# Token-major products written into the recurrence's steps, and Ln with Exp on ScalarE for the powers of three norms

## The chip, the cores and the metric

The kernel runs on one core of a Trainium2 chip, on one sequence of 512 tokens with 1024 features, in float32. The metric is the device time of one execution in microseconds (us); lower is better. A core's engines have queues of their own and each works through its queue in order: PE (TensorE, matrix products; PEld is its loading of weights), DVE (VectorE), ACT (ScalarE), POOL (GpSimd) and SP, which here only starts DMAs. An engine waits for another by semaphores.

## What is computed

Two networks run one after the other, each of two layers. The change concerns the second one, whose layer has a hybrid mixer: sliding-window attention, a gated linear recurrence (`hgrn2`) and a gated delta rule, fed by one projection, and their outputs joined by another. Cut to the norms that the change touches:

```python
def rmsnorm_2(x, gain):          # x / sqrt(mean(x*x) + eps), times (a gain)
def l2norm(x):                   # x / sqrt(sum(x*x) + eps)

def hybrid_mixer(h, ...):
    aq, ak, av, bq, bf, bv, bg, cqkv, cg, cb, ca = jnp.split(h @ w_in, split_at, axis=-1)
    ...                                          # attention on aq, ak, av
    o_b = hgrn2_chunked(bq, log_f, bv)
    out_b = rmsnorm_2(o_b, hgrn_norm) * jax.nn.silu(bg)
    cq, ck, cv = ...                             # silu of a causal convolution of cqkv
    cq = l2norm(cq) * (C_DK ** -0.5)
    ck = l2norm(ck)
    o_c = gated_delta_chunked(cq, ck, cv, beta, g)
    out_c = rmsnorm_2(o_c, gdn_norm) * jax.nn.silu(cg)
    return jnp.concatenate([out_a, out_b, out_c], axis=-1) @ w_out
```

Every one of these norms needs a power -1/2 of a few columns: 128 tokens by 4, 8 or 32 values.

## The kernel before

All activations of a layer stay in the core's memory. Weights stream in by DMA, 128 rows of a matrix at a time (`wraw`). Every large product is made of three products of reduced-precision parts, so that it comes near float32: ACT casts the weights to a high part `whi` (L381), DVE subtracts it to get the low part `wlo` (L382), and PE adds up high times high (L406), low times high (L407) and high times low (L408) in one accumulator. Feature-major products (features on partitions, `lin_f`) do this for one output tile of 128 features with 24 matmuls of 512 columns; the token-major ones (tokens on partitions, `lin_t`, lines L475 to L477) do it with the activations as the moving side. A scheduler sets the order on each engine: it takes operations in the order in which they are written, as a priority, but lets later ones go ahead where its model of the time says that an earlier one would wait. The program that comes out is fixed; the queues don't reorder it.

One hybrid layer is written out by `second_mixer` (L1707 to L1771). It makes four feature-major tiles, then starts the recurrence (`hgrn`, a generator whose steps the caller asks for) between the 512-column token-major products of `win2_t0`; runs the steps to their end; makes the 392-column products of `win2_t1` (their results leave by `evt1`, L1741); makes the five tiles of queries and keys for the attention (each is evicted as `u` at L1721, squared at L663, and the square summed by eight two-column products at L1724); makes six tiles for the delta rule, with a causal convolution and a tanh (L832 to L844); and then weaves the delta rule (`gdn`) with the attention (`swa`). The output projection, `w_out`, follows; its first input tiles are ready early, and its products fill PE beside the delta rule's last blocks.

Three norms take their power on POOL:

- The recurrence's output norm: `hgrn` calls `head_rstd` (L1019) for each of two pairs of heads. ACT copies the result out of PSUM (`ho`, L1332) and squares it (`hsq`, L1024), DVE sums and scales it (`hms`, L1026, L1030), POOL raises 8 columns to -1/2 (`pw`, L669), and DVE multiplies (L1334, L1335).
- The norms of the delta rule's queries and keys: PE sums squares with two-column products (L1379), DVE adds the epsilon (`gms`, L1381), POOL raises three groups of columns (`grn`, L1384); ACT spreads them over 64 columns each (`sp`, L682), PE transposes the spread (L676), and DVE multiplies the two key tiles with it (L1390). The queries' part goes into `grq` (L1394).
- The delta rule's output norm, once for each of four blocks of 128 tokens: `hsq` on ACT, `hms` on DVE (L1026 to L1030, with `grq` squared into it), the power of 4 columns on POOL (L669), two products on DVE (L1033, L1567), and two transposes on PE (L1569) that put the block into the tiles from which the output projection's last inputs are cast (`hi`, L399).

Of the kernel before, what the change touches and what calls it, by code (L numbers as in the profile page):

```python
# [12 lines left out]
AF = mybir.ActivationFunctionType  # L13
ALU = mybir.AluOpType
# [3 lines left out]
P = 128  # L18
SEQ = 512
NB = SEQ // P  # L20
# [229 lines left out]
class Net:  # L250
# [415 lines left out]
    def pow_half(self, x, n):  # L666
# [2 lines left out]
        self.nc.gpsimd.tensor_tensor(r, x, self.nhalf[:, 0:n], op=ALU.pow)  # L669
        return r  # L670

    def spread(self, cols):

        ps = self.ps()
        for b in range(NB):
            self.nc.tensor.transpose(ps[:, b * P:(b + 1) * P], cols(b), self.ident)  # L676
        return ps
# [338 lines left out]

        last.append(lambda: finish(*late.pop(0), "mm"))

    def head_rstd(self, x, shape, pre=None):  # L1019

        V = self.nc.vector
        a, b = shape
        sq = self.t((P, a, b, 64), name="hsq")
        self.nc.scalar.activation(out=sq, in_=x, func=AF.Square)  # L1024
        ms = self.small((P, a, b), f"hms{a}{b}", 2)
        V.tensor_reduce(ms, sq, axis=AX.X, op=ALU.add)  # L1026
        if pre is not None:
            V.tensor_tensor(ms, ms, pre, op=ALU.mult)
            V.tensor_tensor(ms, ms, pre, op=ALU.mult)
        V.tensor_scalar(ms, ms, 1.0 / 64, EPS, op0=ALU.mult, op1=ALU.add)  # L1030
        r = self.pow_half(ms.rearrange("p a b -> p (a b)"), a * b).rearrange("p (a b) -> p a b", a=a)
        if pre is not None:
            V.tensor_tensor(r, r, pre, op=ALU.mult)  # L1033
        return r
# [175 lines left out]
    def hgrn(self, q, z, v, bg, l, last):  # L1210
        nc, V, G = self.nc, self.nc.vector, self.nc.gpsimd
# [38 lines left out]
        def pair(i):  # L1250
# [79 lines left out]
                        nc.tensor.matmul(o, w, x, start=n == 0, stop=n == len(terms) - 1)  # L1330
            hs = self.t((P, NB, 2, 64), name="ho")
            nc.scalar.copy(hs, ps.rearrange("p (a b c) -> p b a c", a=2, b=NB))  # L1332
            r = self.head_rstd(hs, (NB, 2))
            V.tensor_tensor(hs, hs, bg[:, :, i * P:(i + 1) * P].rearrange("p a (b c) -> p a b c", b=2), op=ALU.mult)  # L1334
            V.tensor_tensor(hs, hs, r.unsqueeze(3).to_broadcast([P, NB, 2, 64]), op=ALU.mult)  # L1335
            done[i] = hs
# [9 lines left out]
    def gdn(self, x, cg, ba, l, out):  # L1346
        nc, V, G = self.nc, self.nc.vector, self.nc.gpsimd
# [20 lines left out]
        f = lambda y: y.rearrange("p a b -> p (a b)")  # L1368
# [10 lines left out]
                T.matmul(st[:, 8 * b + 2 * i:8 * b + 2 * i + 2], sq[:, b * P:(b + 1) * P], self.bd64[:, 0:65:64], start=True, stop=True)  # L1379
        rs_ = self.small((P, 32), "gms", 2)  # L1380
        V.tensor_scalar(rs_, st[:, 0:32], EPS, None, op0=ALU.add)  # L1381
        rs3, rn = rs_.rearrange("p (a b) -> p a b", a=NB), self.small((P, NB, 8), "grn", 2)
        def power(c):
            G.tensor_tensor(rn[:, :, c], rs3[:, :, c], self.nhalf[:, 0:32].rearrange("p (a b) -> p a b", a=NB)[:, :, c], op=ALU.pow)  # L1384

        power(slice(4, 6))
        power(slice(6, 8))
        for i in range(2, 4):
            ps = early.spread2(rn[:, :, 2 * i:2 * i + 2])
            V.tensor_tensor(x[i], x[i], ps, op=ALU.mult)  # L1390
            yield
        power(slice(0, 4))
        rq = self.small((P, NB, 4), "grq", 2)
        V.tensor_scalar(rq, rn[:, :, 0:4], 0.125, None, op0=ALU.mult)  # L1394
        q, k, vf = x[0:2], x[2:4], x[4:6]
# [147 lines left out]
        for b in range(NB):  # L1543
            s = slice(b * P, (b + 1) * P)
            un, hs = self.t((P, 4, 64), name="gvn", tag="x"), self.t((P, 1, 4, 64), name="go", tag="x")
            po = self.ps("mx")
            o3 = lambda y: y.rearrange("p (a b) -> p a b", a=4)
            if b == 0:
                V.tensor_copy(un, uw[b][:, :, 0:64])
            else:  # L1550
                for i in range(2):
                    T.matmul(po[:, i * P:(i + 1) * P], wt[i][:, s], sbd[b][:, i, :], start=True, stop=True)
                    T.matmul(po[:, 256 + i * P:256 + (i + 1) * P], q[i][:, s], sbd[b][:, i, :], start=True, stop=True)
                V.tensor_tensor(un, uw[b][:, :, 0:64], o3(po[:, 0:256]), op=ALU.subtract)
            p2 = self.ps("mx")
            for h in range(4):
                T.matmul(p2[:, h * 64:(h + 1) * 64], QT[b][:, h, :], un[:, h, :], start=True, stop=True)
            if b == 0:
                V.tensor_copy(hs[:, 0], o3(p2[:, 0:256]))
            else:  # L1560
                t = self.t((P, 4, 64), name="got", tag="x")
                V.tensor_tensor(t, o3(po[:, 256:512]), eg[:, b, :].unsqueeze(2).to_broadcast([P, 4, 64]), op=ALU.mult)
                V.tensor_tensor(hs[:, 0], t, o3(p2[:, 0:256]), op=ALU.add)
            r = self.head_rstd(hs, (1, 4), rq[:, b:b + 1, :])
            h3 = hs[:, 0]
            V.tensor_tensor(h3, h3, o3(cg[:, b, :]), op=ALU.mult)
            V.tensor_tensor(h3, h3, r.rearrange("p a b -> p (a b)").unsqueeze(2).to_broadcast([P, 4, 64]), op=ALU.mult)  # L1567
            for i in range(2):
                T.transpose(yt[i][:, s], h3[:, 2 * i:2 * i + 2, :].rearrange("p a b -> p (a b)"), self.ident)  # L1569
            yield  # L1570
# [136 lines left out]
    def second_mixer(self, x, l):  # L1707
# [47 lines left out]
        for n, _ in enumerate(self.lin_t_steps(self.d["win2_t0"][l], x, 512, evt0)):  # L1755
            if n + 1 in (7, 8):
                next(gh)
        for n, _ in enumerate(gh):
            if n == 2:
                gains(bg, "hgrn_norm")  # L1760
        self.lin_t(self.d["win2_t1"][l], x, 392, evt1)
        gains(cg, "gdn_norm")
        self.lin_f(w[10:15], x, lambda o, ps: ev(o + 10, ps))
        ga = self.using("l", "mx").swa([keep[o] for o in range(10, 14)], keep[14], keep["st"], av, l, self.tab2, y_a)
# [71 lines left out]
def drain(gen):  # L1836
    for _ in gen:
        pass
# [25 lines left out]
```

## Time and profile before

| | |
|---|---|
| time, median of 3 runs | 3589.97 us (3586.79 to 3591.79) |
| profiled execution, its own time | 3586.55 us |
| its span, first to last instruction | 3584.7 us |
| busy: PE, DVE, ACT, POOL | 97%, 55%, 38%, 4% of the span |
| mean granted TensorE clock | 0.992 of full speed |

The span is the recorded stretch of the profiled execution; its time is a little longer by what lies around it. Busy time is an average over stages with different limits, so the views by stretch (windows) and by instruction (timeline) say more than the shares. In the timeline a row may hold several like instructions (x8), and a bracket tells how long the engine had been idle before and what ended that.

### The profile page before, as it was taken

The page shows a single profiled execution, that of the slowest core. Times are in us where ns is not written, and L with a number is a line of the kernel's source. Part 1 is how long each engine was busy: PE and PEld are TensorE (multiplying, and loading weights), DVE is VectorE, ACT ScalarE, POOL GpSimd, SP SyncE. Part 2 cuts the span into 40 slices and gives each one's busy share as a digit, 9 for nine tenths or more (in the row PEclk, how much of TensorE's full clock was granted, in tenths as well). Part 3 has the DMA queues.
Part 4 walks back from the last instruction along what each step waited for, and adds up shares of the span by engine and source line. Part 5 has one row for each costly group of instructions (what it writes and reads, how often), then busy time and mean ns, then how long its engine had stood idle before and what let it go on. Part 6 is the DMA issues. An engine that isn't in the chain of part 4 may idle for free.

```text
span 3584.7 us, 44503 instructions
## 1 busy us (share of the span) xinstructions
PE 3484.3 (97%) x17694; PEld 2901.8 (81%) x17694; DVE 1989.1 (55%) x3074; ACT 1364.5 (38%) x2231; POOL 140.5 (4%) x130
## 2 busy tenths in 40 slices
PE   9999999999999999999999998899999989999999
PEld 7888777888888888777888887788888877888887
DVE  6555665554665555674556577756333475654333
ACT  4223454323333223463223364354222453543221
POOL 0000000000000000000000003100000021000000
PEclk9999999999999999999999999899999999999999
DMA  5444212444334443202444321102333222022332
GB/s 167 141 135 129 84 32 68 142 145 128 127 100 142 146 138 100 91 15 95 146 148 137 94 77 54 62 7 75 108 98 101 78 71 68 1 71 90 100 99 83
DMA packets 114272, 349.06 MB, mean 97 GB/s; under 512 B 11536, under 2 KB 27920, under 8 KB 114064
## 3 DMA queue, kind: packets, MB, share of 16 engines
q1 hardware_dynamic: 114064, 346.21, 30.8%
q8 instruction: 140, 2.29, 0.3%
q14 instruction: 68, 0.56, 0.0%
HBM read 339.87 MB, written 2.10 MB: 95 GB/s over the span
## 4 chain that ended last, share of the span: by engine, by line
PE 87%; DVE 6%; issue 3%; ACT 2%; POOL 1%; DMA 1%; SPq 0%; POOLq 0%; DVEq 0%; ACTq 0%
PE mm L406 24%; PE mm L408 24%; PE mm L407 24%; PE mm L1481 1%; PE mm L1476 1%; PE mm L476 1%; PE mm L477 1%; PE mm L475 1%; PE mx L968 1%; DVE hacc L1279 1%; DVE wlo L382 1%; PE mm L809 1%; PE mx L948 1%; ACT sc L1138 1%; PE mx L1121 1%
## 5 line engine op out<-in xcount | busy, mean ns | idle before, releaser
L381 ACT CAST whi<-wraw 128x1024 fp32r<-128x1024 f32 (+3 forms) x540 | 553.4, 1029 | 1553.6 <-PE mm L407 1271.7
L406 PE MATMUL mm<-xh,whi 128*128 128x512 f32 (+1 forms) x2784 | 1053.3, 380 | 9.7 <-ACT whi L381 6.4
L407 PE MATMUL mm<-xl,whi 128*128 128x512 f32 (+1 forms) x2784 | 1055.8, 380 | 1.6 <-DVE xl L588 1.4
L408 PE MATMUL mm<-xh,wlo 128*128 128x512 f32 (+1 forms) x2784 | 1055.8, 380 | 0.3 <-DVE wlo L382 0.3
L382 DVE TENSOR_TENSOR wlo<-wraw,whi 128x1024 fp32r<-128x1024 f32 (+3 forms) x540 | 643.7, 1194 | 274.9 <-ACT whi L381 234.3
L406 PEld LDWEIGHTS mm<-xh,whi 128*128 128x128 f32 x2784 | 522.4, 189 | 107.8 <-ACT whi L381 6.4
L407 PEld LDWEIGHTS mm<-xl,whi 128*128 128x128 f32 x2784 | 524.9, 189 | 100.3 <-DVE xl L588 2.5
L408 PEld LDWEIGHTS mm<-xh,wlo 128*128 128x128 f32 x2784 | 524.8, 189 | 100.4 <-DVE wlo L382 3.1
L408 PE MATMUL mm<-hi,wlo 128*128 128x512 f32 (+1 forms) x1390 | 532.2, 383 | 2.1 <-DVE wlo L382 2.1
L406 PE MATMUL mm<-hi,whi 128*128 128x512 f32 (+1 forms) x1390 | 532.5, 384 | 0.2
L407 PE MATMUL mm<-lo,whi 128*128 128x512 f32 (+1 forms) x1390 | 531.8, 383 | 0.0
L408 PEld LDWEIGHTS mm<-hi,wlo 128*128 128x128 f32 x1390 | 261.3, 188 | 54.2 <-DVE wlo L382 4.2
L406 PEld LDWEIGHTS mm<-hi,whi 128*128 128x128 f32 x1390 | 261.1, 188 | 51.4 <-ACT hi L399 1.1
L407 PEld LDWEIGHTS mm<-lo,whi 128*128 128x128 f32 x1390 | 261.3, 188 | 50.3
L658 DVE SCALAR_TENSOR_TENSOR h<-mm,h 128x512 f32<-128x512 f32 x112 | 77.2, 691 | 224.2 <-PE mm L408 224.1
L1589 DVE SCALAR_TENSOR_TENSOR ada<-wraw,cond,ada 128x1024 f32<-128x1024 f32 x84 | 107.9, 1284 | 95.6 <-DMA wraw<-in_ada_w_dram 95.2
L637 DVE TENSOR_TENSOR gl<-mm,rstd 128x512 f32<-128x512 f32 x88 | 60.7, 690 | 155.1 <-PE mm L408 155.1
L636 DVE TENSOR_TENSOR silu<-mm,rstd 128x512 f32<-128x512 f32 x88 | 60.7, 689 | 145.2 <-PE mm L408 145.2
L658 DVE SCALAR_TENSOR_TENSOR h<-mm,mod,h 128x512 f32<-128x512 f32 (+1 forms) x70 | 48.9, 704 | 148.7 <-PE mm L408 148.7
L399 ACT CAST hi<-gl 128x512 fp32r<-128x512 f32 x132 | 82.2, 623 | 100.6 <-DVE gl L639 99.9
L633 DVE TENSOR_TENSOR gl<-silu,mm 128x512 f32<-128x512 f32 x44 | 30.2, 687 | 135.8 <-PE mm L408 135.8
L400 DVE TENSOR_TENSOR lo<-gl,hi 128x512 fp32r<-128x512 f32 x132 | 90.5, 686 | 15.4 <-ACT hi L399 15.4
(493 smaller groups left out, 3606.2 us busy)
## 6 DMA issues: line engine op xcount, KB each, us to landing
wraw<-in_ffn_gate_dram SPq DMA_DIRECT2D x130, 512.0 KB, 3.5
wraw<-in_ffn_up_dram SPq DMA_DIRECT2D x130, 512.0 KB, 4.0
wraw<-in_ada_w_dram SPq DMA_DIRECT2D x96, 512.0 KB, 3.7
wraw<-in_ffn_down_dram SPq DMA_DIRECT2D x96, 448.0 KB, 3.3
wraw<-in_win_f_dram SPq DMA_DIRECT2D x50, 512.0 KB, 3.5
wraw<-in_ffn_down_dram SPq DMA_DIRECT2D x48, 512.0 KB, 3.5
wraw<-in_w_out_dram SPq DMA_DIRECT2D x32, 512.0 KB, 3.5
wraw<-in_win_t_dram SPq DMA_DIRECT2D x16, 512.0 KB, 3.5
```

The costliest lines, as they stand in the source:

```text
L381: self.nc.scalar.copy(hi[:, s], raw)
L382: self.nc.vector.tensor_tensor(lo[:, s], raw, hi[:, s].bitcast(F32), op=ALU.subtract)
L399: self.nc.scalar.copy(hi, src)
L400: self.nc.vector.tensor_tensor(lo, src, hi.bitcast(F32), op=ALU.subtract)
L406: T.matmul(ps, whi, xhi, start=first, stop=False)
L407: T.matmul(ps, whi, xlo, start=False, stop=False)
L408: T.matmul(ps, wlo, xhi, start=False, stop=last)
L475: T.matmul(ps, xh[:, bs], w[0][:, s], start=k == 0, stop=False)
L636: nc.vector.tensor_tensor(sg, gate_ps, rb, op=ALU.mult)
L637: nc.vector.tensor_tensor(gg, up_ps, rb, op=ALU.mult)
L658: self.nc.vector.scalar_tensor_tensor(h, ps[:, c], scale, h, op0=ALU.mult, op1=ALU.add)
L1589: V.scalar_tensor_tensor(acc, raw, cond[:, k:k + 1], acc, op0=ALU.mult, op1=ALU.add)
```

## The change

It does two things.

First, the generator of the 392-column products (`t1`) is asked for a step after every second step of the recurrence, and what is left of it is run afterwards. Before, all of it stood behind the recurrence.

Second, a new helper, `exp_half`, computes the power as exp(-ln(x)/2) with two ACT instructions, Ln and Exp with a scale of -0.5. It takes the place of POOL's pow in the three norms above. At the start of the delta rule all 32 columns go through one pair, where POOL had three instructions. `pow_half` stays where other norms use it. ACT's functions come in tables, and the built program has an `ACT_TABLE_LOAD` wherever the next function isn't in the table that is loaded: 29 of them before, 53 after.

```diff
--- before.py
+++ after.py
@@ -667,6 +667,12 @@
 
         r = self.small((P, n), f"pw{n}", 2)
         self.nc.gpsimd.tensor_tensor(r, x, self.nhalf[:, 0:n], op=ALU.pow)
+        return r
+
+    def exp_half(self, x, r):
+
+        self.nc.scalar.activation(out=r, in_=x, func=AF.Ln)
+        self.nc.scalar.activation(out=r, in_=r, func=AF.Exp, scale=-0.5)
         return r
 
     def spread(self, cols):
@@ -1016,7 +1022,7 @@
 
         last.append(lambda: finish(*late.pop(0), "mm"))
 
-    def head_rstd(self, x, shape, pre=None):
+    def head_rstd(self, x, shape, pre=None, power=None):
 
         V = self.nc.vector
         a, b = shape
@@ -1028,7 +1034,10 @@
             V.tensor_tensor(ms, ms, pre, op=ALU.mult)
             V.tensor_tensor(ms, ms, pre, op=ALU.mult)
         V.tensor_scalar(ms, ms, 1.0 / 64, EPS, op0=ALU.mult, op1=ALU.add)
-        r = self.pow_half(ms.rearrange("p a b -> p (a b)"), a * b).rearrange("p (a b) -> p a b", a=a)
+        if power:
+            r = power(ms, self.small((P, a, b), f"hrs{a}{b}", 2))
+        else:
+            r = self.pow_half(ms.rearrange("p a b -> p (a b)"), a * b).rearrange("p (a b) -> p a b", a=a)
         if pre is not None:
             V.tensor_tensor(r, r, pre, op=ALU.mult)
         return r
@@ -1330,7 +1339,7 @@
                         nc.tensor.matmul(o, w, x, start=n == 0, stop=n == len(terms) - 1)
             hs = self.t((P, NB, 2, 64), name="ho")
             nc.scalar.copy(hs, ps.rearrange("p (a b c) -> p b a c", a=2, b=NB))
-            r = self.head_rstd(hs, (NB, 2))
+            r = self.head_rstd(hs, (NB, 2), power=self.exp_half)
             V.tensor_tensor(hs, hs, bg[:, :, i * P:(i + 1) * P].rearrange("p a (b c) -> p a b c", b=2), op=ALU.mult)
             V.tensor_tensor(hs, hs, r.unsqueeze(3).to_broadcast([P, NB, 2, 64]), op=ALU.mult)
             done[i] = hs
@@ -1379,17 +1388,11 @@
                 T.matmul(st[:, 8 * b + 2 * i:8 * b + 2 * i + 2], sq[:, b * P:(b + 1) * P], self.bd64[:, 0:65:64], start=True, stop=True)
         rs_ = self.small((P, 32), "gms", 2)
         V.tensor_scalar(rs_, st[:, 0:32], EPS, None, op0=ALU.add)
-        rs3, rn = rs_.rearrange("p (a b) -> p a b", a=NB), self.small((P, NB, 8), "grn", 2)
-        def power(c):
-            G.tensor_tensor(rn[:, :, c], rs3[:, :, c], self.nhalf[:, 0:32].rearrange("p (a b) -> p a b", a=NB)[:, :, c], op=ALU.pow)
-
-        power(slice(4, 6))
-        power(slice(6, 8))
+        rn = self.exp_half(rs_.rearrange("p (a b) -> p a b", a=NB), self.small((P, NB, 8), "grn", 2))
         for i in range(2, 4):
             ps = early.spread2(rn[:, :, 2 * i:2 * i + 2])
             V.tensor_tensor(x[i], x[i], ps, op=ALU.mult)
             yield
-        power(slice(0, 4))
         rq = self.small((P, NB, 4), "grq", 2)
         V.tensor_scalar(rq, rn[:, :, 0:4], 0.125, None, op0=ALU.mult)
         q, k, vf = x[0:2], x[2:4], x[4:6]
@@ -1561,7 +1564,7 @@
                 t = self.t((P, 4, 64), name="got", tag="x")
                 V.tensor_tensor(t, o3(po[:, 256:512]), eg[:, b, :].unsqueeze(2).to_broadcast([P, 4, 64]), op=ALU.mult)
                 V.tensor_tensor(hs[:, 0], t, o3(p2[:, 0:256]), op=ALU.add)
-            r = self.head_rstd(hs, (1, 4), rq[:, b:b + 1, :])
+            r = self.head_rstd(hs, (1, 4), rq[:, b:b + 1, :], self.exp_half)
             h3 = hs[:, 0]
             V.tensor_tensor(h3, h3, o3(cg[:, b, :]), op=ALU.mult)
             V.tensor_tensor(h3, h3, r.rearrange("p a b -> p (a b)").unsqueeze(2).to_broadcast([P, 4, 64]), op=ALU.mult)
@@ -1755,10 +1758,14 @@
         for n, _ in enumerate(self.lin_t_steps(self.d["win2_t0"][l], x, 512, evt0)):
             if n + 1 in (7, 8):
                 next(gh)
+
+        t1 = self.lin_t_steps(self.d["win2_t1"][l], x, 392, evt1)
         for n, _ in enumerate(gh):
             if n == 2:
                 gains(bg, "hgrn_norm")
-        self.lin_t(self.d["win2_t1"][l], x, 392, evt1)
+            if n % 2:
+                next(t1, None)
+        drain(t1)
         gains(cg, "gdn_norm")
         self.lin_f(w[10:15], x, lambda o, ps: ev(o + 10, ps))
         ga = self.using("l", "mx").swa([keep[o] for o in range(10, 14)], keep[14], keep["st"], av, l, self.tab2, y_a)
```

How the built program's order moves is shown at three places, all in the first hybrid layer; the second has the same. In the rows a name's number tells buffers apart, and line numbers of the changed kernel are 3 to 9 higher.

**ACT, end of the recurrence.** Before: squares of the two head pairs (`ho` to `hsq`), a weight cast, and the eviction and square of the first query tile (`u`, `sq`).

```order
L1024 ACTIVATE hsq_16496<-ho_16494 128x512
L1332 COPY ho_16526<-mx_16505 128x512
L1024 ACTIVATE hsq_16528<-ho_16526 128x512
L381 CAST whi_16935<-wraw_16933 128x1024
L1721 ACTIVATE u_16749<-mm_16724,vecs 128x512
L663 ACTIVATE sq_16751<-mm_16724 128x512
```

After, from the second `ho` on (`hrs` is the power of `hms`):

```order
L1341 COPY ho_16667<-mx_16646 128x512
L674 ACTIVATE hrs_3133_16641<-hms_3132_16638 128x8
L1030 ACTIVATE hsq_16669<-ho_16667 128x512
L675 ACT_TABLE_LOAD
L675 ACTIVATE hrs_3133_16641<-hrs_3133_16641 128x8
L381 CAST whi_16937<-wraw_16935 128x1024
L674 ACT_TABLE_LOAD
L674 ACTIVATE hrs_3138_16674<-hms_3137_16671 128x8
L1724 ACTIVATE u_16751<-mm_16726,vecs 128x512
L675 ACT_TABLE_LOAD
L675 ACTIVATE hrs_3138_16674<-hrs_3138_16674 128x8
L663 ACTIVATE sq_16753<-mm_16726 128x512
```

Four short instructions and three loads have come ahead of `sq`.

**DVE, start of the delta rule.** Before, from the last step of a convolution to `grq`; L1390 are the products with the spread norm:

```order
L1126 TENSOR_REDUCE wm_17265<-sc_17269 128x2
L841 SCALAR_TENSOR_TENSOR cacc_17130<-conv_17128,vecs,cacc_17130 128x511
L1390 TENSOR_TENSOR cout_17053<-cout_17053,mm_17239 128x512
L1390 TENSOR_TENSOR cout_17094<-cout_17094,mm_17259 128x512
L844 SCALAR_TENSOR_TENSOR cout_17135<-cout_17135,cacc_17130 128x512
L837 TENSOR_SCALAR cacc_17171<-conv_17169,vecs 128x512
L1394 TENSOR_SCALAR grq_17273<-grn_17234 128x16
```

After; here the first of these products is L1394, and `sc` are scores of the attention, `geb` and `grq` small factors:

```order
L847 SCALAR_TENSOR_TENSOR cacc_17132<-conv_17130,vecs,cacc_17132 128x511
L1407 TENSOR_TENSOR geb_17286<-gb_17181,geg_17201 128x16
L1133 TENSOR_TENSOR sc_17306<-mx_17303,mats_16876 128x512
L1397 TENSOR_SCALAR grq_17274<-grn_17236 128x16
L1133 TENSOR_TENSOR sc_17327<-mx_17324,mats_16876 128x512
L1135 TENSOR_REDUCE wm_17267<-sc_17306 128x2
L1135 TENSOR_REDUCE wm_17267<-sc_17327 128x2
L850 SCALAR_TENSOR_TENSOR cout_17137<-cout_17137,cacc_17132 128x512
L843 TENSOR_SCALAR cacc_17173<-conv_17171,vecs 128x512
L1133 TENSOR_TENSOR sc_17343<-mx_17340,mats_16876 128x512
L847 SCALAR_TENSOR_TENSOR cacc_17173<-conv_17171,vecs,cacc_17173 128x509
L1394 TENSOR_TENSOR cout_17055<-cout_17055,mm_17241 128x512
```

Ten other operations have moved between the convolution's step and the first product with the norm.

**ACT and PE, tail of the delta rule.** Before, ACT has the squares of the four blocks and then the casts for the output projection:

```order
L1024 ACTIVATE hsq_18413<-go_18404 128x256
L1024 ACTIVATE hsq_18443<-go_18428 128x256
L1024 ACTIVATE hsq_18473<-go_18458 128x256
L1024 ACTIVATE hsq_18503<-go_18488 128x256
L399 CAST hi_18517<-mx_18401 128x512
L399 CAST hi_18521<-mx_18402 128x512
```

After, its first two blocks and the start of the third:

```order
L1030 ACTIVATE hsq_18414<-go_18405 128x256
L674 ACT_TABLE_LOAD
L674 ACTIVATE hrs_3509_18421<-hms_3508_18416 128x4
L675 ACT_TABLE_LOAD
L675 ACTIVATE hrs_3509_18421<-hrs_3509_18421 128x4
L1030 ACTIVATE hsq_18445<-go_18430 128x256
L674 ACT_TABLE_LOAD
L674 ACTIVATE hrs_3517_18452<-hms_3516_18447 128x4
L675 ACT_TABLE_LOAD
L675 ACTIVATE hrs_3517_18452<-hrs_3517_18452 128x4
L1030 ACTIVATE hsq_18476<-go_18461 128x256
```

Each block's square now stands behind the Exp of the block ahead.

PE before, from the transposes of the third block (L1569) over those of the fourth to the projection's next input tile:

```order
L1569 MATMUL mx_18401<-base,go_18458 128x128
L1569 MATMUL mx_18402<-base,go_18458 128x128
L406 MATMUL mm_18550<-hi_17954,whi_18533 128x512
L407 MATMUL mm_18550<-lo_17955,whi_18533 128x512
L408 MATMUL mm_18550<-hi_17954,wlo_18534 128x512
L406 MATMUL mm_18551<-hi_17954,whi_18539 128x512
L407 MATMUL mm_18551<-lo_17955,whi_18539 128x512
L408 MATMUL mm_18551<-hi_17954,wlo_18540 128x512
L406 MATMUL mm_18552<-hi_17954,whi_18545 128x512
L1569 MATMUL mx_18401<-base,go_18488 128x128
L1569 MATMUL mx_18402<-base,go_18488 128x128
L407 MATMUL mm_18552<-lo_17955,whi_18545 128x512
```

PE after, the same (transposes are L1572 here):

```order
L406 MATMUL mm_18557<-hi_17955,whi_18550 128x512
L407 MATMUL mm_18557<-lo_17956,whi_18550 128x512
L1572 MATMUL mx_18402<-base,go_18461 128x128
L1572 MATMUL mx_18403<-base,go_18461 128x128
L408 MATMUL mm_18557<-hi_17955,wlo_18551 128x512
L1572 MATMUL mx_18402<-base,go_18492 128x128
L1572 MATMUL mx_18403<-base,go_18492 128x128
L406 MATMUL mm_18554<-hi_18522,whi_18532 128x512
L406 MATMUL mm_18555<-hi_18522,whi_18538 128x512
```

Of the seven products between the third and the fourth block's transposes, and the two behind, one is left between and none behind; the others, and two from ahead of the third block, stand ahead now. Further up, 13 products stood between the scores of the first block and its transposes, and now 21.

## Rows read from the trace of the kernel before

**Rows 1.** Page, part 1: busy us (share of the span) x instructions.

```profile
PE 3484.3 (97%) x17694; PEld 2901.8 (81%) x17694; DVE 1989.1 (55%) x3074; ACT 1364.5 (38%) x2231; POOL 140.5 (4%) x130
```

**Rows 2.** Windows view: stretch, length; busy PE, PEld, DVE, ACT, POOL; clock, DMA.

```profile
2160.00:2215.00 55.00, 45.19 (x386) 37.03 (x386) 53.35 (x80) 19.92 (x49) 24.28 (x19) 1.00 0.12 39
...
2287.00:2335.00 48.00, 37.82 (x234) 32.71 (x233) 40.00 (x102) 21.73 (x59) 6.54 (x3) 0.79 0.08 26
...
2428.00:2450.00 22.00, 19.70 (x112) 15.52 (x111) 11.40 (x40) 2.75 (x6) 4.03 (x4) 1.00 0.00 1
```

**Rows 3.** Waits of PE, 2160 to 2215: total us, times, longest.

```profile
PE mx L1273 <- DVE hk L1265: 8.0, 12, 2.6
```

**Rows 4.** Timeline of ACT: start, us, engine, line, operation, [idle before <-releaser].

```profile
2216.51 0.22 ACT L852 ACTIVATE gla<-gla 128x16 f32<-128x16 f32 x1
...
2216.74 1.28 ACT L853 ACT_TABLE_LOAD   x1
...
2218.04 0.31 ACT L853 ACTIVATE gla<-gla,one 128x16 f32<-128x16 f32 x1
```

**Rows 5.** Timeline, end of the recurrence, beside the query products.

```profile
2230.71 1.05 ACT L381 CAST whi<-wraw 128x1024 fp32r<-128x1024 f32 x1 [1.32 <-PE mm L407]
...
2231.66 0.68 ACT L1721 ACTIVATE u<-mm,vecs 128x512 f32<-128x512 f32 x1
...
2232.24 0.59 ACT L663 ACTIVATE sq<-mm 128x512 f32<-128x512 f32 x1
...
2232.34 0.39 PE L407 MATMUL mm<-xl,whi 128*128 128x512 f32 x1
...
2232.56 0.39 PE L408 MATMUL mm<-xh,wlo 128*128 128x512 f32 x1
...
2232.89 1.05 PE L1724 MATMUL mx<-base,sq 128*128 128x2 f32 x8
```

**Rows 6.** Timeline, start of the delta rule: power and spread.

```profile
2296.30 6.54 POOL L1384 TENSOR_TENSOR grn<-gms,nhalf 128x8 f32<-128x8 f32 x3 [34.67 <-DVE gms L1381]
...
2298.41 0.62 ACT L682 COPY sp<-grn 128x512 f32<-128x512 f32 x1 [6.29 <-POOL grn L1384]
...
2299.08 1.12 PE L676 MATMUL mm<-base,sp 128*128 128x128 f32 x4 [2.54 <-ACT sp L682]
...
2300.24 0.69 DVE L1390 TENSOR_TENSOR cout<-cout,mm 128x512 f32<-128x512 f32 x1 [2.37 <-PE mm L676]
...
2301.91 0.69 DVE L1390 TENSOR_TENSOR cout<-cout,mm 128x512 f32<-128x512 f32 x1 [0.98 <-PE mm L676]
```

**Rows 7.** Timeline, tail of the delta rule: power, transposes, out-projection.

```profile
2430.49 1.01 POOL L669 TENSOR_TENSOR pw<-hms,nhalf 128x4 f32<-128x4 f32 x1 [9.86 <-DVE hms L1030]
...
2431.54 0.16 DVE L1033 TENSOR_TENSOR pw<-pw,grq 128x4 f32<-128x4 f32 x1 [1.13 <-POOL pw L669]
...
2432.22 0.44 PE L1569 MATMUL mx<-base,go 128*128 128x128 f32 x2 [0.94 <-DVE go L1567]
...
2439.55 0.44 PE L1569 MATMUL mx<-base,go 128*128 128x128 f32 x2
...
2443.12 0.44 PE L1569 MATMUL mx<-base,go 128*128 128x128 f32 x2 [0.15 <-DVE go L1567]
...
2446.30 0.44 PE L1569 MATMUL mx<-base,go 128*128 128x128 f32 x2 [1.11 <-DVE go L1567]
...
2447.30 1.19 PE L406 MATMUL mm<-hi,whi 128*128 128x512 f32 x4
```

**Rows 8.** Timeline of PE (two rows) and windows view (two rows): the clock.

```profile
2162.88 1.16 PE L1273 MATMUL mx<-hq,hk 64*128 64x128 f32 x16 [2.55 <-DVE hk L1265]
...
2287.55 2.82 PE L1379 MATMUL mm<-base,sq 128*128 128x2 f32 x24
...
2291.00:2295.00 4.00, 4.00 (x12) 3.25 (x11) 1.79 (x4) 0.90 (x3) 0.00 (x0) 0.57 0.37 132
...
2298.40:2312.05 13.65, 7.89 (x31) 6.43 (x32) 10.78 (x20) 5.24 (x9) 4.44 (x2) 0.50 0.00 1
```

## The prediction

> **What bounds the kernel now.** I read the page's line of engine shares first. PE is busy 97% of the span [rows 1], so an edit on another engine counts only where PE waits for it, or would. Then the stages of one hybrid layer [rows 2]. In the recurrence (2160 to 2215) PE is busy 45.19 of 55 us and DVE 53.35: DVE is the bound. At the start of the delta rule (2287 to 2335) PE has 37.82 of 48, at its tail (2428 to 2450) 19.70 of 22. Between the first two PE is full. The other hybrid layer shows the same pattern about 737 us later, so every term is worked out for one layer and doubled. The rest of the program, the first network included, is untouched. Last I read, instruction by instruction, the places where a power is taken [rows 5 to 7].
>
> **Interleaving: nothing.** The row to save is PE waiting 8.0 us in 12 pieces on DVE's hk products [rows 3]; 16.0 us in both layers. But the order on PE through the recurrence is the same row for row before and after: the scheduler already puts the 392-column products where a step leaves PE free, and when they are written doesn't alter that. DVE stays full [rows 2]. Cost 0; bounds of 1 us either way, for two small exponentials that change place with one cast.
>
> **The power, in general.** POOL's pow goes (1.01 us for 4 columns, 6.54 for the three at the delta start [rows 6, 7]), and two ScalarE instructions come. A short one takes 0.22 us (0.31 for 16 columns), a table load 1.28 [rows 4]. The built program has a load before the Ln and another before the Exp, in nearly every pair. A load waits for nothing, so the one ahead of Ln runs while ACT waits for the mean square; the one between Ln and Exp can't be hidden, and whatever stands behind in ACT's in-order queue pays for both. A pair therefore costs 0.22 + 1.28 + 0.22 = 1.72 us, plus gaps of 0.02.
>
> The Trainium skill ("ScalarE: Activation LUTs", section "What ACT_TABLE_LOAD costs") puts 1283 ns on a load, which the row shows, and some 1380 ns of drain on top. The row doesn't show that: one instruction ends at 2216.73, the load starts at 2216.74, and the Ln starts 0.02 us after the load's end [rows 4].
>
> **Place A: the recurrence's norm, beside the query products.** Now ACT does the second hsq, idles 1.32 us until a weight buffer is free, casts (2230.71), evicts u (2231.66), squares (2232.24); then PE takes the square into the eight two-column products of L1724 (2232.89) without having waited: its last two matmuls began at 2232.34 and 2232.56, and the next full one could have begun 0.22 to 0.23 later [rows 5]. After, the first Ln stands ahead of the second hsq; load and Exp stand ahead of the cast; load and Ln ahead of u; load and Exp ahead of the square. That is 3 loads of 1.30 with their gaps and 4 short ones of 0.22: 4.78 us ahead of the square, of which the idle 1.32 swallows part: 3.46. PE has one more matmul ahead of L1724 now, 0.23. So PE, which waits for nothing there now, stands still for 3.2 us. DVE's wait for the second power is longer too, but covered by work that is needed a whole product later. Bounds 2.0 (a load less on the path) and 3.5. All that follows on PE up to the delta rule is dense, so nothing gives this back: **+3.2**.
>
> **Place B: start of the delta rule.** After the mean square POOL works 6.54 us from 2296.30; PE waits 2.54 us for the first spread (2299.08), DVE 2.37 and 0.98 for the two products with it [rows 6]. After: Ln at 2296.3, load, Exp done near 2298.1, all 32 columns at once. The q half of the norm comes some 4 us sooner. But the tanh and the copy of a convolution stand ahead of the two spreads on ACT, so the k half comes no sooner (first spread near 2299.1, where it started at 2298.4), and on DVE ten other operations, half of them from behind it, now stand ahead of L1390. DVE's 3.35 us of waiting can be filled with work that it did later, and DVE is what PE waits for in this stage. Bounds: -4 (both idles and a little PE time at half clock saved), +1 (L1390 some 2 us later, and the copies of k behind it). I take the middle of what the two idles could bring: **-2**.
>
> **Place C: tail of the delta rule.** Four blocks follow each other: hsq on ACT, mean on DVE, power, two products on DVE, transposes L1569 on PE. DVE waits 1.13 us for POOL here [rows 7]; the pair takes 1.72 and its handover, 1.85. Also hsq of the next block now stands behind the Exp of this one. I walk the blocks with durations of the rows. Block 0: Ln at 2430.49, where pow began; Exp ends 2432.2; transposes could start at 2432.95. But eight matmuls more stand ahead of them, 1.82 us, begun where PE now idles 0.94: 2433.1 against 2432.22, +0.88. Block 1: everything 0.88 later, plus a pair for a pow, 0.72 and a little: 2441.19 against 2439.55, +1.64. Block 2: its hsq could come at 2439.8 and waits for block 1's Exp until 2440.45, then another pair: 2445.25 against 2443.12, +2.13. Block 3 the same way: 2448.87 against 2446.30, +2.57 [rows 7]. The casts and the products L406 x4 of the out-projection follow as now, 1.00 us later: 2449.87 against 2447.30 [rows 7]. PE has no work to put there: before the last transposes seven matmuls stood between them and the ones before; now one, and none behind. So the end moves by the whole chain: **+2.6**. Bounds 2.0 (three blocks by 0.66) and 3.6 (0.88 and four times 0.7).
>
> **The clock.** After places A and C PE runs dense code, and there the clock matters. TensorE fell from 2.4 to 1.2 GHz after 2.82 us of two-column products at 2287.55 without a gap: mean 0.57 of full speed between 2291 and 2295 [rows 8], that is (1 - 0.57) / 0.5 x 4 = 3.4 us at half. It fell again after the 2.54 us wait at 2296.5, 0.50 for 13.65 us; but it didn't fall after 2.55 us of idling before 2162.88: the recurrence is at 1.00 [rows 2, 6, 8]. At A, PE would idle 3.2 us and then do 1.05 us of two-column products; at C idle 3.2 us, do two transposes, and idle 0.8. Both are longer than any of these stretches, so I expect a fall after each. 3.4 us at half clock costs up to 1.7 us where PE is dense: **+1.5 each**, bounds 0 and 1.7.
>
> **Sum.** A layer: 3.2 + 1.5 - 2 + 2.6 + 1.5 = 6.8; two layers **+13.6 us**. The profiled execution took 3586.55 us, of which 3584.7 are the span; the rest doesn't change. It lies 3.42 us under the median, 3589.97, which I take as the base: 3603.6, rounded to **3603.5 us**. What this kernel's measurement can tell from no change is about 0.2%, 7.2 us.
>
> **Rivals.**
> The clock stays up at A and C. For it: the recurrence idles 2.55 us in one piece without a fall [rows 8]. Against it: A and C are longer, and thin work stands beside the wait. 2 x (3.2 - 2 + 2.6) = +7.6: 3597.6, right at the edge of what can be told.
> Not slower: the delta start pays for the rest. The mechanism is DVE's 3.35 us of waiting for POOL [rows 6]: if all of it is filled, and the stretch at half clock ends sooner with it, B gives 4 a layer; with no clock fall at A and C the sum is 2 x (3.2 - 4 + 2.6) = +3.6: 3593.6, within 0.2%. From 2.2 a layer without falls (5.2 with them) it is no longer slower. Against it: L1390, the step that waited, comes later after the change.
> The interleaving works after all and PE's waits in the recurrence go: 16.0 us less [rows 3] than the forecast, 3587.5, and under 3583 with the better end of B. Against it: PE's order there is unchanged and DVE is full.
> One load serves Ln and Exp. Then the loads of A and C fall away: a pair takes 0.44, less than pow's 1.01 [rows 7], A adds nothing, C gives about 0.6 three times, B 2.5: 2 x (-4.3) = -8.6, 3581. Against it: the built program has a load row for both. The Trainium skill ("ScalarE: Activation LUTs", section "Table sets: the hidden batching unit") says that one set holds both functions and one load does; the order of this program doesn't use that.
> A load empties the engine first, and each of the seven unhidden loads of A and C costs more than 1.28. The gap of 0.02 us around it [rows 4] speaks against it; were a load to cost double, 2 x 7 x 1.28 = +18 more: 3621. With the drain of the page above the sum would be an estimated 19 us more.
>
> **How the numbers follow.** Forecast (a fall at one or both places, B between 0 and -3): 0.59, all slower. Clock stays up: 0.20, half slower, half within 0.2%. Delta start pays: 0.11, within. Interleaving: 0.04, of which 0.03 faster. One load: 0.03, faster. Dearer loads: 0.03, slower. That makes slower 0.72, within 0.22, faster 0.06. Range 3594.5 to 3610: down to where the second and third case lie, up to A and C at their high bounds with full clock costs and 0.5 of gain at B, 2 x (3.5 + 1.7 + 3.6 + 1.7 - 0.5) = 20; it leaves out the last two cases, interleaving and part of the delta start.
>
> **What would show it.** The recurrence (2160 to 2215) with the same PE busy time. At L1724 a PE wait of about 3.2 us for the square on ACT. At the delta start DVE without the two waits for L676, and the stage about 2 us shorter. In the tail L1569's waits grow, with 3 us ahead of the last one. Half-clock windows behind L1724's first group and behind L406 x4. The prediction is wrong if loads are hidden at A, if the scheduler's order gives PE other work than I read, or if the stage from 2287 to 2335 shrinks by more than 4 us.

## The result

The changed kernel takes 3606.99 us (median of 4; 3604.53 to 3610.78), the kernel before 3588.42 in the same comparison: a ratio of 1.0055, 95% interval 1.0042 to 1.0067, so it is slower by 15 to 24 us. The ratio makes 19.7 us; the medians lie 18.6 apart. The profiled execution of the changed kernel took 3604.53 us, its span is 3602.7 us: 18.0 more than before.

The page's engine shares of the changed kernel; PE's busy time has grown by 10 us with as many instructions, POOL has lost 27.5 us and ACT gained 37 [rows 1]:

```profile
PE 3494.7 (97%) x17694; PEld 2911.0 (81%) x17694; DVE 1988.7 (55%) x3074; ACT 1401.2 (39%) x2283; POOL 113.0 (3%) x112
```

**Place A, the recurrence's norm.** The timeline of the changed kernel, ACT from the second `ho` to the square, then PE's group of two-column products that needs it (start, us, engine, line):

```profile
2228.22 0.63 ACT L1030 ACTIVATE hsq<-ho 128x512 f32<-128x512 f32 x1
2228.88 1.28 ACT L675 ACT_TABLE_LOAD   x1
2230.17 0.21 ACT L675 ACTIVATE hrs<-hrs 128x8 f32<-128x8 f32 x1
2230.29 1.04 ACT L381 CAST whi<-wraw 128x1024 fp32r<-128x1024 f32 x1
2231.34 1.28 ACT L674 ACT_TABLE_LOAD   x1
2232.64 0.21 ACT L674 ACTIVATE hrs<-hms 128x8 f32<-128x8 f32 x1
2232.75 0.67 ACT L1724 ACTIVATE u<-mm,vecs 128x512 f32<-128x512 f32 x1
2233.44 1.28 ACT L675 ACT_TABLE_LOAD   x1
2234.73 0.21 ACT L675 ACTIVATE hrs<-hrs 128x8 f32<-128x8 f32 x1
2234.85 0.58 ACT L663 ACTIVATE sq<-mm 128x512 f32<-128x512 f32 x1
...
2235.48 1.86 PE L1727 MATMUL mx<-base,sq 128*128 128x2 f32 x8 [2.84 <-ACT sq L663]
```

The three loads stand where the order had them, and each begins within 0.03 us of the end of the instruction ahead of it. PE waits 2.84 us for the square where it waited for nothing [rows 5]. From the group before to this one it takes 8.07 us, before 4.95.

**Place B, the start of the delta rule.** The timeline there; the first row of DVE is the product with the spread norm, L1390 before [rows 6]:

```profile
2301.47 0.23 ACT L674 ACTIVATE grn<-gms 128x32 f32<-128x32 f32 x1 [2.83 <-DVE gms L1390]
2301.72 1.28 ACT L675 ACT_TABLE_LOAD   x1
...
2303.01 0.23 ACT L675 ACTIVATE grn<-grn 128x32 f32<-128x32 f32 x1
...
2303.92 3.75 PE L1130 MATMUL mx<-kz,u 128*128 128x256 f32 x8 [2.16 <-DVE sc L1133]
...
2304.13 1.14 ACT L688 COPY sp<-grn 128x512 f32<-128x512 f32 x2
...
2307.46 1.91 PE L682 MATMUL mm<-base,sp 128*128 128x128 f32 x8
2308.56 0.69 DVE L1394 TENSOR_TENSOR cout<-cout,mm 128x512 f32<-128x512 f32 x1 [0.68 <-PE mm L682]
```

The power is ready 1.8 us after Ln begins, and DVE's wait for the spread norm has shrunk from 3.35 us to 0.68. But the first product with the norm comes 7.1 us after the power's begin, before 3.9. PE no longer waits for the spread; it waits 2.16 us for DVE's scores now.

**Place C, the tail.** The last block on ACT and DVE, then the four pairs of transposes and the projection's next products [rows 7]:

```profile
2452.09 0.20 ACT L674 ACTIVATE hrs<-hms 128x4 f32<-128x4 f32 x1 [0.22 <-DVE hms L1036]
2452.32 1.28 ACT L675 ACT_TABLE_LOAD   x1
2453.61 0.20 ACT L675 ACTIVATE hrs<-hrs 128x4 f32<-128x4 f32 x1
...
2453.84 0.16 DVE L1042 TENSOR_TENSOR hrs<-hrs,grq 128x4 f32<-128x4 f32 x1 [1.79 <-ACT hrs L675]
...
2439.04 0.41 PE L1572 MATMUL mx<-base,go 128*128 128x128 f32 x2
2447.01 0.44 PE L1572 MATMUL mx<-base,go 128*128 128x128 f32 x2 [0.61 <-DVE go L1570]
2450.98 0.44 PE L1572 MATMUL mx<-base,go 128*128 128x128 f32 x2 [0.54 <-DVE go L1570]
2454.52 0.69 PE L1572 MATMUL mx<-base,go 128*128 128x128 f32 x2 [2.87 <-DVE go L1570]
2455.67 2.07 PE L406 MATMUL mm<-hi,whi 128*128 128x512 f32 x4 [0.46 <-ACT hi L399]
```

DVE waits 1.79 us for the power (1.13 to 1.19 before), and from the first transposes to the last it takes 15.48 us, before 14.08. PE stands still for 2.87 us ahead of the last.

**The clock.** The windows view of the changed kernel, behind A, further behind A, and behind C (the number after the five busy times is the granted clock):

```profile
2234.00:2242.00 8.00, 6.52 (x20) 5.52 (x21) 0.69 (x1) 1.42 (x3) 0.00 (x0) 0.57 0.17 61
2242.00:2246.00 4.00, 4.00 (x23) 3.20 (x22) 1.23 (x1) 2.12 (x3) 0.00 (x0) 1.00 0.09 10
...
2453.50:2461.50 8.00, 6.52 (x19) 4.92 (x20) 1.94 (x5) 1.67 (x5) 0.00 (x0) 0.59 0.00 0
```

At both places TensorE falls to 1.2 GHz: 0.57 over 8 us is (1 - 0.57) / 0.5 x 8 = 6.9 us at half, and 0.59 is 6.6. The product behind A takes 9.19 us from group to group in the first layer, 7.94 in the second, before 6.59 and 6.60: +2.60 and +1.34.

### The profile page after: what moved, and what is told of

The parts are those of the page before. It is cut to its first block, busy times and chain, and to the rows that moved or that the text cites. A ratio compares the mean times of both kernels' runs of the same rounds, so it can differ in the third digit from the quotient of the medians.

```text
span 3602.7 us, 44537 instructions
## 1 busy us (share of the span) xinstructions
PE 3494.7 (97%) x17694; PEld 2911.0 (81%) x17694; DVE 1988.7 (55%) x3074; ACT 1401.2 (39%) x2283; POOL 113.0 (3%) x112
## 4 chain that ended last, share of the span: by engine, by line
PE 87%; DVE 5%; issue 3%; ACT 2%; POOL 1%; DMA 0%; SPq 0%; POOLq 0%; DVEq 0%; ACTq 0%
PE mm L406 25%; PE mm L408 24%; PE mm L407 24%; PE mm L1484 1%; PE mm L1479 1%; PE mm L476 1%; PE mm L477 1%; PE mx L974 1%; PE mm L475 1%; DVE hacc L1288 1%; PE mx L1130 1%; DVE wlo L382 1%; PE mm L815 1%; PE mx L954 1%; PE mx L1339 1%
## 5 line engine op out<-in xcount | busy, mean ns | idle before, releaser
L408 PEld LDWEIGHTS mm<-xh,wlo 128*128 128x128 f32 x2784 | 526.2, 189 | 100.5 <-DVE wlo L382 3.0
```

The source lines that it names most:

```text
L408: T.matmul(ps, wlo, xhi, start=False, stop=last)
```

## Experiments

Each is measured against the kernel before, run on the same chip. A table of four stages, in us, first and second hybrid layer, from the starts of the rows in each timeline. "A wait": from the first to the second group of two-column products of the query tiles; "A next": to the third; "B": from the last two-column sums of the q and k norms to the first product of the delta rule's matrices (gk with cout); "C": from the first to the last transposes of the tail.

| kernel | A wait | A next | B | C | ratio to before (95%) |
|---|---|---|---|---|---|
| before | 4.95, 4.94 | 6.59, 6.60 | 36.64, 36.56 | 14.08, 14.07 | |
| changed | 8.07, 8.06 | 9.19, 7.94 | 34.95, 34.44 | 15.48, 15.49 | 1.0055 (1.0042 to 1.0067) |
| interleaving alone | 4.94, 4.94 | 6.58, 6.60 | 36.56, 36.35 | 14.08, 14.08 | 1.0000 (0.9992 to 1.0009) |
| start alone | 4.94, 4.94 | 6.60, 6.55 | 34.62, 36.46 | 14.08, 14.08 | 1.0001 (0.9992 to 1.0009) |
| recurrence alone | 8.07, 8.06 | 7.94, 7.94 | 36.32, 36.63 | 14.08, 14.08 | 1.0029 (1.0018 to 1.0039) |
| tail alone | 4.94, 4.92 | 6.59, 6.59 | 36.56, 36.96 | 15.48, 15.47 | 1.0024 (1.0016 to 1.0033) |
| three powers, no interleaving | 8.07, 8.06 | 9.53, 9.53 | 34.57, 34.57 | 15.47, 15.48 | 1.0043 (1.0028 to 1.0058) |
| one Ln and Exp for two pairs | 6.58, 6.57 | 6.36, 7.93 | 36.65, 37.01 | 14.07, 14.08 | 1.0015 (1.0005 to 1.0025) |

**Interleaving alone.** The edit is the first part of the diff by itself.

> Only the interleaving; every power stays on POOL. Theory (the interleaving changes no order that matters): the time of before, within 0.1%, and the recurrence's stage from PE's long wait on hk to the first group of two-column query products takes 65.1 to 66.4 us as before. Rival (the interleaving is what made that stage 2.0 us longer in the first layer of the changed kernel): +2 us or more in that stage, and about +2 to +4 us in the whole.

The ratio is 1.0000. The stage from the long wait on hk to the first group takes 65.09 and 66.54 us, before 65.06 and 66.44. The PE waits of the recurrence (total us, times, longest), next to [rows 3]:

```profile
PE mx L1273 <- DVE hk L1265: 6.6, 8, 2.6
```

The longest is the same 2.6. The sum is 1.4 us lower, but the stage isn't shorter: PE is busy 58.95 us in it instead of 57.65, at a granted clock of 0.97 instead of 1.00. So nothing that the interleaving does can be told in the time. The changed kernel took 67.0 us in this stage in its first layer, 2 more than before, at a clock of 0.95 (0.66 from 2206 to 2216). That isn't the interleaving's doing: the run with the tail alone, whose recurrence is that of before, took 66.9 and 68.5 us, at 0.95 and 0.93.

**Start alone.** `exp_half` is called only for `grn`; both calls of `head_rstd` keep POOL.

> Ln and Exp only at the start of the delta rule, no interleaving, POOL for the other norms. Theory (the start gains 1.7 to 2.1 us a layer, as between the traces of before and after): 3.4 to 4.2 us less than before, 0.1%. Rival (the gain came only because PE arrived later or the clock stood otherwise in the changed kernel): 0, or some us more.

The time stays: 1.0001, so the 3.4 to 4.2 us are out, though a smaller gain isn't (the interval ends 0.08%, 2.9 us, below). The stage gained 2.0 us in the first layer and 0.1 in the second. PE's waits in the stage, first layer:

```profile
PE mm L1453 <- DVE ge L1444: 3.1, 1, 3.1
PE mm L719 <- DVE cout L850: 2.6, 1, 2.6
PE mx L1130 <- DVE sc L1133: 2.2, 1, 2.2
```

The wait for the spread (3.0 us in all before) is gone, but 7.9 us of waits for DVE stand there, before 9.5 us of waits of all kinds. The two windows of the stage, first and second layer, show the rest:

```profile
2295.92:2330.54 34.62, 26.65 (x167) 23.03 (x166) 32.76 (x85) 19.43 (x50) 0.00 (x0) 0.85 0.01 1
3033.93:3070.39 36.46, 27.97 (x168) 24.24 (x166) 32.85 (x85) 19.44 (x50) 0.00 (x0) 0.81 0.00 1
```

Same work, but PE needs 1.3 us more in the second, at a mean clock of 0.81 against 0.85, and DVE waits 4.6 us for it instead of 3.2. Over all kernels that take this power on ScalarE, the stage lasts between 34.4 and 36.5 us (mean of ten 35.0); with POOL between 36.3 and 37.1 (mean of fourteen 36.7).

**Recurrence alone.** `exp_half` only in the call of `hgrn`.

> Ln and Exp only in the recurrence's norm. Theory (three loads stand ahead of the square): PE waits about 2.85 us for the square at the second group of two-column products, group to group 8.07 us instead of 4.95, and the clock falls there and costs 1.3 to 2.6 us: +9 to +11 us in both layers. Rival (the clock falls for another reason, such as the start or the tail): only the stall, +6.2 us, and no stretch at half clock behind it.

1.0029, that is +10.4 us (6.5 to 14.0). Two rows of PE, the group ahead and the one that waits, and the window behind it:

```profile
2227.13 1.00 PE L1733 MATMUL mx<-base,sq 128*128 128x2 f32 x8
2235.20 1.05 PE L1733 MATMUL mx<-base,sq 128*128 128x2 f32 x8 [2.85 <-ACT sq L663]
...
2235.00:2241.00 6.00, 5.80 (x23) 4.79 (x24) 0.39 (x1) 0.19 (x2) 0.00 (x0) 0.72 0.07 30
```

The wait is that of the changed kernel, and the clock falls behind it with nothing else changed: (1 - 0.72) / 0.5 x 6 = 3.4 us at half, which cost 1.35 us in each layer. By the stages 2 x (3.12 + 1.35) = 8.9.

**Tail alone.** `exp_half` only in the call of `gdn`'s output norm.

> Ln and Exp only in the output norm of the delta rule. Theory (four blocks in a chain): the first product of the last input tile comes 2.35 us later a layer, and a fall of the clock behind it costs 2.1 to 2.7 us: +9 to +10 us in both layers. Rival (the products of the projection fill the time, and the shift of before to after came from the clock that fell earlier): under +5 us.

1.0024, +8.6 us (5.7 to 11.8). Transposes of the four blocks and the window behind:

```profile
2432.78 0.42 PE L1578 MATMUL mx<-base,go 128*128 128x128 f32 x2
2440.75 0.44 PE L1578 MATMUL mx<-base,go 128*128 128x128 f32 x2 [0.61 <-DVE go L1576]
2444.71 0.44 PE L1578 MATMUL mx<-base,go 128*128 128x128 f32 x2 [0.54 <-DVE go L1576]
2448.26 0.44 PE L1578 MATMUL mx<-base,go 128*128 128x128 f32 x2 [2.87 <-DVE go L1576]
...
2449.00:2454.00 5.00, 4.74 (x14) 3.75 (x15) 1.29 (x2) 0.69 (x2) 0.00 (x0) 0.66 0.00 0
```

The same waits as in the changed kernel, to the hundredth, and a fall behind them, (1 - 0.66) / 0.5 x 5 = 3.4 us. The three parts alone add to 10.4 + 0.4 + 8.6 = 19.4 us, each known to some 3 or 4 us either way; the whole change is +0.55%, 19.7.

**Three powers without interleaving.** The second part of the diff by itself.

> All three powers on ScalarE, no interleaving. Theory (the parts add up and the interleaving is nothing): the time of the changed kernel, +0.55% on before, 17 to 20 us; group to group 8.07 us at the query products, 15.48 us from the first to the last transposes of the tail. Rival (the interleaving costs part of it): 2 to 4 us less than the changed kernel, and the recurrence's stage 65 to 66.5 us in both layers.

1.0043 (1.0028 to 1.0058), 15 us. That is 4 us under the whole change, or 3 by the medians, as the rival has it, but the two intervals overlap, and the rival's other sign fails: the recurrence takes 66.9 us in both layers, not 65 to 66.5. With the interleaving alone at 1.0000 (at most 0.09% dearer, 3 us), the difference isn't shown to be more than noise. A's wait, B and C are those of the changed kernel.

**Sums one product later.** The whole change, and this edit in the query tiles' eviction, which puts 14 more matmuls ahead of the products that need the square:

```diff
-            for b in range(NB):
-                nc.tensor.matmul(keep["st"][...], sq[:, b * P:(b + 1) * P], ...)
+            def sums():
+                for b in range(NB):
+                    nc.tensor.matmul(keep["st"][...], sq[:, b * P:(b + 1) * P], ...)
+            for f in held:
+                f()
+            held[:] = [sums] if o < 14 else []
+            if o == 14:
+                sums()
```

> The changed kernel, but the eight two-column products of a query tile are written one product later, so that PE has 14 more matmuls (3.2 us) to do before it needs the square. Theory (at the recurrence's norm the cost is PE's wait for the square and the fall of the clock behind it): both go, 2.85 us to at most 0.3 us of wait and no stretch at half clock there, about 9 to 11 us less than the changed kernel, +0.25 to +0.3% on before. Rival (ScalarE's three loads delay something else too, such as the next product's weights): a wait of 1.5 us or more appears elsewhere within the next two products.

1.0010 (1.0000 to 1.0019): 16 us of the 20 are gone, more than expected; the same edit on the kernel before changes nothing that can be told (0.9997, below). ACT's three loads are all still there, and no wait for the square is left (groups of PE, and the window from the first of them to the delta rule):

```profile
2230.22 0.95 PE L1728 MATMUL mx<-base,sq 128*128 128x2 f32 x8
2236.60 0.95 PE L1728 MATMUL mx<-base,sq 128*128 128x2 f32 x8
2242.99 0.95 PE L1728 MATMUL mx<-base,sq 128*128 128x2 f32 x8
...
2228.00:2290.00 62.00, 60.68 (x311) 51.29 (x310) 40.15 (x70) 25.53 (x41) 7.65 (x2) 1.00 0.28 87
```

The clock stays at 1.00. So A is the wait of one PE instruction and the fall behind it, not ACT's time. The two profiled executions, this kernel's and the changed one's, differ by 16.8 us. Of these, 12.3 lie between the long wait on hk and the fifth group of two-column products, both layers together: A was 3.12 + 2.60 and 3.12 + 1.34 there, 10.2, and the period of a query product is 6.39 us where before it was 6.58. Another 3.4 us aren't shown to be the edit's. At the start of the delta rule, 24 two-column products were followed by a fall to 0.57 in the kernel before [rows 8]; here none follows, in either layer, and the last such sums come 5.80 us after the first instead of 7.49:

```profile
2287.00:2295.00 8.00, 7.40 (x55) 6.90 (x54) 6.20 (x16) 4.41 (x9) 0.00 (x0) 1.00 0.49 149
```

That fall is missing in the second layer with the interleaving alone and with one Ln and Exp too, and it stands in both layers of the last run below (sums later, start on ScalarE), which has this edit. How much of the 16 us it makes over all executions isn't known.

**One Ln and one Exp for two head pairs.** Only the recurrence's norm is on ScalarE; the mean squares of both pairs go into one tile, and one `exp_half` behind both takes the two powers.

```diff
-            r = self.head_rstd(hs, (NB, 2), power=self.exp_half)
+            ...                                # square and mean into both[:, i]
...
         yield from weave(pair(0), pair(1))
+        r = self.exp_half(both, self.small((P, 2, NB, 2), "hrsb", 2))
```

> Ln and Exp only in the recurrence's norm, but one Ln and one Exp for both head pairs, so that one load stands ahead of the square instead of three. Theory (each load costs its 1.28 us and a gap there, nothing is drained): ScalarE pays 1.28 + 2 x 0.22 and gaps, 1.7 to 1.8 us, ahead of the square; PE waits 1.2 to 1.6 us instead of 2.85, group to group 6.4 to 6.7 us. Whether the clock falls behind it is open; without a fall +3 us in both layers, with one +6. Rival (a load costs double by a drain): PE waits 2.6 us or more.

One load instead of three on the path; PE waits 1.35 and 1.36 us. The two layers' rows and the windows behind them:

```profile
2236.97 1.05 PE L1740 MATMUL mx<-base,sq 128*128 128x2 f32 x8 [1.35 <-ACT sq L663]
...
2975.96 1.05 PE L1740 MATMUL mx<-base,sq 128*128 128x2 f32 x8 [1.36 <-ACT sq L663]
...
2236.00:2243.00 7.00, 6.04 (x31) 5.13 (x31) 2.05 (x3) 2.75 (x6) 0.00 (x0) 1.00 0.21 75
2976.00:2983.00 7.00, 7.00 (x28) 5.76 (x29) 0.96 (x3) 1.29 (x2) 0.00 (x0) 0.76 0.14 53
```

The ratio makes 5.4 us, between the two cases of the theory. Against before, the load, the Ln and the Exp made the interval 1.63 us longer (6.58 against 4.95), which leaves no room for a second cost of a load. Against three loads it is 1.49 us shorter and not 2.6 or more, since ACT idles 1.31 us ahead of its cast again, which the loads had filled. The same wait was followed by a fall in one layer and by none in the other.

**A doubled power in the tail.** The tail alone, with Ln, Exp, Ln, Exp for each power.

> The tail alone on ScalarE, with Ln, Exp, Ln, Exp for each power: two more loads and two more short instructions, 3.0 us a block. Theory (the four blocks are one chain, whose length goes to the end): the last transposes come 9 to 12 us later a layer than with one pair, so +18 to +24 us on the run with one pair. Rival (PE's products of the projection cover part of it): under +12 us.

3622.78 us in a single execution, so without an interval: 24.9 above the median of the tail alone, a little over the 18 to 24 expected. The rows of the four transposes:

```profile
2439.09 0.44 PE L1580 MATMUL mx<-base,go 128*128 128x128 f32 x2 [2.60 <-DVE go L1578]
2452.15 0.44 PE L1580 MATMUL mx<-base,go 128*128 128x128 f32 x2 [3.01 <-DVE go L1578]
2458.49 0.69 PE L1580 MATMUL mx<-base,go 128*128 128x128 f32 x2 [3.22 <-DVE go L1578]
2465.07 0.69 PE L1580 MATMUL mx<-base,go 128*128 128x128 f32 x2 [5.89 <-DVE go L1578]
```

From the first to the last 26.0 us, and 24.5 in the second layer, against 15.5: +10.5 and +9.0, and the first comes 3.0 us later too, counted from the first product of the delta rule's matrices. The four blocks are one chain; nothing that PE has left covers it.

**Two tries at a better kernel.** The sums one product later with all powers on POOL, and the same with the start on ScalarE.

> The kernel before, with only the sums of squares of the query tiles written one product later, all powers on POOL. In the changed kernel with this edit the period from group to group was 6.39 us where before has 6.58. Theory (each group of two-column products lost 0.1 us to a wait for the square and 0.1 to its place): 0.19 us for each of four products and what the last one gains, 1 to 2 us a layer, 0 to -0.1% on before. Rival (the saving stood in a clock that happened to be up): 0.

> The same, and Ln with Exp at the start of the delta rule alone. Over the traces so far that stage takes 35.0 us (mean of 8) with Ln and Exp and 36.6 us (mean of 12) with POOL, so 1.6 us a layer. Theory: 3 us less than the run with the sums alone, -0.1 to -0.2% on before. Rival (a change of clock elsewhere gives it back, as where the start alone was changed and the time stayed): no difference between the two.

Both give 0.9997 (0.9989 to 1.0006 and 0.9988 to 1.0006): no difference that can be told. The period of a query product is 6.39 us in both, 0.19 less than before, and the start takes 34.44 and 36.01 us in the second, 37.09 and 37.05 in the first. The second kernel gains 3.7 us there, but in the profiled executions the two falls behind the 24 two-column products, which only it has, take 3.3 of them back (7.48 and 7.46 us from the first to the last sums, against 5.80).

## Why the forecast held, step by step

- **Interleaving 0.** Right, by the run with it alone, within 3 us. That PE's busy time in the recurrence would stay didn't come out in every layer: 57.65 to 60.22 us in the first, with the clock at 0.95 instead of 1.00. In its rival, 16.0 us less together with the better end of B is 3583.5 and not "under 3583".
- **Place A, +3.2 a layer.** Measured 3.12 in both layers and in each kernel that has it. The loads ahead of the square and the idle time that swallows part of them were what sized it; with one load the interval grew by 1.63 only.
- **The clock behind A, +1.5.** Right that it falls, by the run with the recurrence alone; its size was 1.35 where it fell for 3.4 us, and 2.6 to 2.9 where it fell for 6.8, beyond the bound of 1.7 that I took from the one stretch in [rows 8]. How long the falls are was the part of the clock terms that went wrong.
- **Place B, -2.** The waits for POOL went, and the stage was 1.69 and 2.12 us shorter in the changed kernel, 1.6 to 1.7 on the mean of all traces, though the first product with the norm came 3.2 us later, not 2. But alone it brought nothing that can be measured in the time (2.9 us less to 3.2 more): in one layer of two, PE's clock and DVE's waits for PE gave back what it brought. So the term is near what the stage shows, and it isn't shown that the whole gets it; that the stage's gain depends on how the clock falls in it is read from two windows and isn't tested by itself.
- **Place C, +2.6.** First transposes +0.9 (in the tail-alone run 102.5 to 102.8 us after the first product of the delta rule's matrices, before 101.8 in the second layer; before's first layer has 100.5, so the size is good to about 1 us), first to last +1.40: 2.3. The walk through the blocks was right, with each of its three steps 0.1 us too long.
- **The clock behind C, +1.5.** It falls in every kernel with this power in the tail; in the changed kernel it cost 2.1 us behind the first layer and 2.7 behind the second, as far as the next landmark shows.
- **Sum.** +13.6 forecast, about 19 measured. The range held it, since it allowed for full clock costs at both places; the middle was 4.4 us under the 18.0 of the profiled executions. The two clock terms were 2.7 too small (+1.5 each; in the changed kernel 2.60 and 1.34 behind A, 2.1 and 2.7 behind C), and 2.3 lie in stretches that the forecast had at nothing. Two layers of A, B and C by the table and the clock behind C give 10.2 - 3.8 + 4.6 + 4.7 = 15.7 in the profiled execution; the other 2.3 of its 18.0 lie elsewhere: stretches at half clock in the first layer (in the recurrence, and 0.57 from 2340 to 2348) cost some 4.4 more, against 2.5 less ahead of the first recurrence. Such stretches come and go from trace to trace, so that part of the sum isn't shown to belong to the change.
- **Rivals.** That the clock stays up fell with the two windows. That the start pays for the rest fell with the start alone. Loads that cost double fell with the run with one load, which agrees with the gap of 0.02 us in [rows 4]. One load for Ln and Exp isn't what the program has: its rows show both.

## What to carry to other kernels

A function on ScalarE that isn't in the loaded table is paid by what stands behind it in ScalarE's queue, so count the loads between the new instruction and the next one that PE needs, not the time of the function itself. Where PE needs a small result soon, look at how many of its instructions stand in between: moving eight two-column products behind 14 more matmuls took away four fifths of what this change cost; the wait and the fall behind it are the part that is shown to be its work. In the recurrence and the tail, a pow on an engine that has nothing else to do, at 1.64 us for 8 columns and 1.0 for 4, was cheaper than 0.4 us of work and a load on one that others wait for.

## What was not expected of the hardware

The same PE wait, 2.84 to 2.85 us, was followed by 3.4 us at half clock in the run with the recurrence alone and in the second layer of the changed kernel, and by 6.8 us in the first layer of the changed kernel and both layers without interleaving. In these three the clock had fallen before the end of the wait or in the first half microsecond of the eight two-column products, which took 1.70 to 1.86 us; in the others they still ran at full clock, in 1.05, and the fall came behind them. A wait of 1.35 us was followed by 3.4 us in one layer and by none in the other. So the price of a stall in a dense stretch was its length and between 0 and 2.9 us more, and what decides between them was not settled here. It is no different without a wait: 24 two-column products without a gap were followed by a fall in both layers of the kernel before, and by none in both layers of the changed kernel with the sums later.
